# A SwiGLU layer's down projections issued one pair of up projections later, with the last one added on the vector engine

## The chip, the cores and the metric

The kernel runs on one core of one Trainium2 chip. A core has a tensor engine (PE; its weight loads are shown apart as PEld), a vector engine (DVE), a scalar engine (ACT), GpSimd (POOL) and SyncE (SP), which run side by side and wait for one another by semaphores; SP and POOL issue the DMAs here. The metric is the device time of one execution in microseconds (us), as the median of several.

## The reference

One decoder layer of 512 tokens, model width 1024 and FFN width 2816, all in float32. The change touches the two feed-forward parts, the first and the last of the four:

```python
def swiglu(x, w1, w3, w2):
    return (jax.nn.silu(x @ w1) * (x @ w3)) @ w2
...
h = layer_norm(ALPHA * h + 0.5 * swiglu(h, ffn1_w1, ffn1_w3, ffn1_w2), ln1_g, ln1_b)
h = layer_norm(ALPHA * h + parallel_mixer(h, ...), ln2_g, ln2_b)
h = layer_norm(ALPHA * h + memory_attention(h, mem, ...), ln3_g, ln3_b)
h = layer_norm(ALPHA * h + 0.5 * swiglu(h, ffn2_w1, ffn2_w3, ffn2_w2), ln4_g, ln4_b)
```

## The kernel before

**Numbers.** Each float32 operand is split into a high part (a CAST to fp32r) and a low part (source minus high part), so each weight tile costs a CAST of 128x1024 on ACT or DVE and a TENSOR_TENSOR of 128x1024 on DVE. One product of two split operands is three matmuls (`mm3`).

**The seven products.** The FFN width is cut into 22 tiles of 128, in 11 pairs. An **up unit** (`seven`) computes the gated activations G of a pair; a **down unit** (`down7`) multiplies four tiles, that is pairs 2g and 2g+1, by their rows of w2. Both are 2x2 block products done with seven block products in place of eight (a Strassen-Winograd scheme). An up unit is 7 products of 24 matmuls of 256 columns (tiles `pxwp`, `pzwp`, `pywp`), a down unit 7 products of 12 matmuls of 512 columns (`dx`, `dy`, `dz`). The weights of a product are formed on chip: four block additions on DVE (`wp_b`, `wd_b`) and seven splits per unit (`wp_hl`, `wd_hl`).

**Forms.** The other operand of a down product is a form `A1` to `A7` of G: blocks of G as they stand for 1, 2 and 4 (A1 from pair 2g, A2 and A4 from pair 2g+1), and the sums `Sa`, `Sb`, `Sc`, `Sd` for 5, 6, 3 and 7, each split like a weight. `Sa` is a block of pair 2g+1 minus one of pair 2g.

**Order of the work.** Pair 0 is done in plain form first, pair 10 goes through `res.add` (the last down projection, the residual and the layer norm; PE tile `res_w`). Between them, five groups: up 2g, up 2g+1, down g (group 0 has no first up). Down g therefore comes right behind the up unit whose G its forms A2 and A5 need.

**Accumulation.** A down unit's products leave PSUM through ACT (`st<-dx`, two copies for each result) and are added into four DRAM arrays `acc` by POOL's DMAs with accumulation; the first unit instead adds to the old residual on DVE and writes it by SP. Before `res.add` the sum is read back from DRAM into SBUF by eight SP DMAs (`load_acc`).

**Who decides the order on an engine.** PE's order follows the generators: each `yield` hands over to others, and what PE needs is pushed out before it. ACT, DVE and POOL get their rows from `Issue`, which keeps pending operations with a modelled cost and time and leaves the one whose data are due first; CASTs may go to ACT or DVE, whichever is modelled to end first. Weight splits get a delay of 4000 ns (`LATER`) in that due time. The order is fixed when the program is built. Split weights live in five buffers (`wsplit`), so the sixth is filled once the first was used.

The lines that set the groups and form A1 and A2 ahead of the down unit, and A5 and A6 at its start:

```python
        for g in range(5):
            if g:
                yield from seven(2 * g)
            forms = Forms(g)
            yield from seven(2 * g + 1, {4: lambda: forms.make(1, 2)})
            yield from down7(g, forms)
```

Of the kernel before, what the change touches and what calls it, by code (L numbers as in the profile page):

```python
# [13 lines left out]
ALU = mybir.AluOpType  # L14
# [180 lines left out]
def layer(ctx: ExitStack, tc: tile.TileContext, a: dict, out: bass.AP):  # L195
# [13 lines left out]
    act, dve, pool, sp = (Timed(issue, getattr(nc, e), e) for e in ("scalar", "vector", "gpsimd", "sync"))  # L209

    def slot(name, dtype=F32R, shape=None):
        return arena.tile(shape or [P, 2, 512], dtype, tag="slot", name=name)
# [39 lines left out]
    def split(hi, lo, src, scale=None):  # L252
        scaled(hi, src, scale)
        if scale is None:
            dve.tensor_tensor(lo, src, f32(hi), op=ALU.subtract)
        else:
            dve.scalar_tensor_tensor(lo, src, scale, f32(hi), op0=ALU.mult, op1=ALU.subtract)
# [105 lines left out]
    def project(name, w, toks=slice(None), o=0):  # L363

        ps = bank(name)
        for k in range(KT):
            mm3(ps, hl_of(w, slice(o + k * P, o + (k + 1) * P)), hk(k, toks), k == 0, k == KT - 1)
            if k % 2 and k < KT - 1:
                yield
        return ps  # L370
# [181 lines left out]
    def products(name, sums, out, late={}):  # L552

        def product(ps, i, first):
            late.get(i, lambda: None)()
            hl = W.take(f"{name}_{i}")
            for w in range(2):
                for k in range(4):  # L560
                    o = w * 512 + k * P
                    mm3(ps[:, w * 256:(w + 1) * 256], hl_of(hl, slice(o, o + P)), sums[i](k),
                        first and w == 0 and k == 0, w == 1 and k == 3, not first)
            W.done(f"{name}_{i}")

        x = bank(f"px{name}")
        product(x, 1, True)
        p1 = wk(f"p1_{name}")
        act.copy(p1, x)
        yield  # L570
        z = bank(f"pz{name}")
        product(z, 5, True)
        p5 = wk(f"p5_{name}")
        act.copy(p5, z)
        yield
        product(x, 6, False)
        u2 = wk(f"u2_{name}")
        act.copy(u2, x)
        yield
        product(z, 3, False)  # L580
        dve.tensor_tensor(u2, u2, z, op=ALU.add)
        drop(z)
        out(1, 0, u2, -1.0)
        yield
        product(x, 7, False)
        dve.tensor_tensor(p5, p5, x, op=ALU.add)
        out(1, 1, p5, -1.0)
        yield
        y = bank(f"py{name}")
        product(y, 2, True)  # L590
        dve.tensor_tensor(p1, p1, y, op=ALU.add)
        drop(y)
        out(0, 0, p1, 1.0)
        yield
        product(x, 4, False)
        out(0, 1, x, 1.0)
        drop(x)
        yield

    def plan_ffn(n, w1, w3, w2):  # L600
        for f in range(2):
            W.plan(f"w1_{n}_{f}", w1[f])
            W.plan(f"w3_{n}_{f}", w3[f])

        def up(p):
            return Unit(f"wp{n}_{p}", [[w[2 * p + i % 2][:, i // 2 * 512:i // 2 * 512 + 512] for w in (w1, w3)] for i in range(4)], ORDER)

        def down(g):
            return Unit(f"wd{n}_{g}", [[w2[f * P:(f + 1) * P, i % 2 * 512:i % 2 * 512 + 512] for f in (4 * g + i // 2 * 2, 4 * g + i // 2 * 2 + 1)]
                                       for i in range(4)], DOWN)  # L610

        units = [up(1), down(0)]
        for g in range(1, 5):
            units += [up(2 * g), up(2 * g + 1), down(g)]
        units.append(up(10))
        for u, v in zip(units, units[1:]):
            u.after = v
        for u in units:
            u.plan()
        for f in (20, 21):  # L620
            W.plan(f"w2_{n}_{f}", w2[f * P:(f + 1) * P])

    def ffn(n, src, ready=None):
        res = Residual(n, src)
# [7 lines left out]
        def gated(f, pa, pb):  # L632
            if f // 2 not in raw:
                raw[f // 2] = slot(f"G{n}_{f // 2}", F32)
            s = raw[f // 2][:, f % 2]
            act.activation(s, pa, AF.Silu)
            dve.scalar_tensor_tensor(s, pb, 0.5, s, op0=ALU.mult, op1=ALU.mult)
            drop(pa, pb)

        def up(fs):  # L640
            for f in fs:
                ps = []
                for w in ("w1", "w3"):
                    key = f"{w}_{n}_{f}"
                    ps.append((yield from project(f"p{key}", W.take(key))))
                    W.done(key)
                    yield
                gated(f, *ps)

        def seven(p, late=()):  # L650

            gated = raw[p] = slot(f"G{n}_{p}", F32)

            def out(c, half, ps, sign):
                dst = gated[:, c, 256 * half:256 * half + 256]
                act.activation(dst, ps[:, :256], AF.Silu, scale=sign)
                dve.scalar_tensor_tensor(dst, ps[:, 256:], 0.5 * sign, dst, op0=ALU.mult, op1=ALU.mult)
                if half and p == 10:
                    f = 2 * p + c
                    gT[f] = slot(f"g{n}_{f}")  # L660
                    split(gT[f][:, 0], gT[f][:, 1], gated[:, c])

            return products(f"wp{n}_{p}", sums, out, dict(late))
# [36 lines left out]
        def load_old():  # L700
            for h in range(2):
                for c in range(2):
                    t = old[h, c] = slot(f"old{n}_{h}_{c}", F32)
                    sp.dma_start(t, rows(src[256 * h:256 * h + 256, c * 512:c * 512 + 512]))

        def down7(g, forms):

            def product(pss, i, first):
                hl, x = W.take(f"wd{n}_{g}_{i}"), forms.hl.pop(i)
                for t in range(2):  # L710
                    for k in range(2):
                        mm3(pss[t], [x[:, k, j, t * P:(t + 1) * P] for j in (0, 1)], hl_of(hl, slice(k * 512, k * 512 + 512)),
                            first and k == 0, k == 1, not first)
                W.done(f"wd{n}_{g}_{i}")

            def add(pss, h, c, sign, new=False):
                if g == 0 and new:
                    st = old.pop((h, c))
                    for t in range(2):
                        dve.scalar_tensor_tensor(st[:, t], st[:, t], ALPHA, pss[t], op0=ALU.mult, op1=ALU.add if sign > 0 else ALU.subtract)  # L720
                    sp.dma_start(rows(acc[h, c]), st)
                else:
                    st = slot(f"st{n}_{g}_{h}_{c}", F32)
                    for t in range(2):
                        act.activation(st[:, t], pss[t], AF.Copy, scale=sign)
                    pool.dma_start(rows(acc[h, c]), st, accum_op=ALU.add)

            x = [bank(f"dx{n}_{g}_{t}") for t in range(2)]
            product(x, 1, True)
            add(x, 0, 0, 1.0, True)  # L730
            forms.make(5, 6)
            yield
            y = [bank(f"dy{n}_{g}_{t}") for t in range(2)]
            product(y, 2, True)
            add(y, 0, 0, 1.0)
            drop(*y)
            forms.make(3)
            yield
            z = [bank(f"dz{n}_{g}_{t}") for t in range(2)]
            product(z, 5, True)  # L740
            add(z, 1, 1, -1.0, True)
            forms.make(7)
            yield
            product(x, 6, False)
            add(x, 0, 1, -1.0, True)
            forms.make(4)
            yield
            product(z, 3, False)
            add(z, 0, 1, -1.0)
            drop(*z)  # L750
            yield
            product(x, 7, False)
            add(x, 1, 1, -1.0)
            yield
            product(x, 4, False)
            add(x, 1, 0, 1.0, True)
            drop(*x)
            yield
# [8 lines left out]
            mark = sums_of_h(n, sums)  # L767
            yield from up(range(2))
        yield mark
        load_old()  # L770
        for g in range(5):
            if g:
                yield from seven(2 * g)
            forms = Forms(g)
            yield from seven(2 * g + 1, {4: lambda: forms.make(1, 2)})
            yield from down7(g, forms)

        def load_acc():
            res.acc = [slot(f"acc{n}_{t}", F32, [P, D]) for t in range(NT)]
# [1 line left out]
                for c in range(2):  # L781
                    sp.dma_start(res.acc[t][:, c * 512:c * 512 + 512], acc[t // 2, c][t % 2 * P:t % 2 * P + P])

        yield from seven(10, {7: load_acc})
        yield from res.add(lambda i, t: hl_of(gT[20 + i], slice(t * P, (t + 1) * P)), [f"w2_{n}_{f}" for f in (20, 21)], False, True)


# [707 lines left out]
```

## Time and profile before

| | |
|---|---|
| median of 3 runs | 1308.88 us (1308.3 to 1309.8) |
| profiled execution, its own time | 1306.86 us |
| its span | 1305.0 us |
| mean granted clock of TensorE | 0.987 |
| PE busy | 1229.0 us, 94% of the span |
| DVE busy | 1038.6 us, 80% |
| ACT busy | 551.3 us, 42% |
| POOL busy | 99.4 us, 8% |

The busy shares are means over stages of different kinds. The first FFN runs from about 34 to 390 us, the second from about 955 us to the end; the mixer and the memory attention lie between and are not changed. A busy PE is one that has matmuls in flight; a gap between the records, with the name of what ended it, is a wait.

### The profile page before, as it was taken

Reading aid. Unit: us, or ns where it says so; the run is one execution under the profiler, and the core shown is the slowest. Engines: PE = TensorE matmul, PEld = TensorE weight load, DVE = VectorE, ACT = ScalarE, POOL = GpSimd, SP = SyncE. Lnnn points to the kernel's source line nnn. Section 1 sums busy time; section 2 is a strip of 40 time slices with the busy share of each in tenths; the row PEclk is TensorE's granted clock in tenths of the full one; section 3 lists DMA queues with packets and bytes.
Section 4 is the critical chain, followed back from the end, with each engine's and each line's share of the span. In section 5 each row is a group of like instructions: output and inputs, shape, how many; then the busy total and the mean of one; then the engine's idle time right before and its main releaser. Section 6 shows DMA issues by size and latency. Waiting matters only on the chain.

```text
span 1305.0 us, 19366 instructions
## 1 busy us (share of the span) xinstructions
PE 1229.0 (94%) x7530; PEld 1079.6 (83%) x7530; DVE 1038.6 (80%) x1603; ACT 551.3 (42%) x977; POOL 99.4 (8%) x95
## 2 busy tenths in 40 slices
PE   7898989899969999999999999999998989899995
PEld 6898988788859987877778898888996979797975
DVE  8999898789873699666666684574999898998987
ACT  5253434353532377433441243451544353535352
POOL 0010202020201100000000000000001020202020
PEclk9999999899989999999999999999999999999998
DMA  9381929484853321242333445234735474748374
GB/s 335 124 261 39 256 61 216 101 198 110 154 177 94 110 72 33 62 133 85 94 98 97 178 162 161 67 128 161 253 118 152 156 182 126 194 114 203 104 127 147
DMA packets 82879, 184.14 MB, mean 141 GB/s; under 512 B 8259, under 2 KB 10051, under 8 KB 82788
## 3 DMA queue, kind: packets, MB, share of 16 engines
q1 hardware_dynamic: 65924, 150.40, 34.3%
q0 software_dynamic: 16864, 32.51, 14.9%
q8 instruction: 59, 0.97, 0.3%
q14 instruction: 32, 0.26, 0.1%
HBM read 137.13 MB, written 45.74 MB: 140 GB/s over the span
## 4 chain that ended last, share of the span: by engine, by line
PE 70%; DVE 19%; DMA 4%; ACT 3%; issue 3%; SPq 0%; POOL 0%; DVEq 0%; POOLq 0%; ACTq 0%
PE pxwp L260 13%; PE pzwp L260 7%; DVE wd_hl L178 6%; PE dx L260 6%; PE dz L260 4%; PE mq L260 3%; PE res_w_o L260 3%; PE pgd L260 3%; PE res_mem_w_o L260 3%; DVE wd_b L178 2%; PE pywp L260 2%; PE pw L260 2%; PE mk L260 2%; PE vd L260 2%; PE pw_gm L260 2%
## 5 line engine op out<-in xcount | busy, mean ns | idle before, releaser
L178 DVE TENSOR_TENSOR wp_hl<-wp_b,wp_hl 128x1024 fp32r<-128x1024 f32 x140 | 168.9, 1222 | 15.6 <-ACT wp_hl L178 14.7
L178 ACT CAST wp_hl<-wp_b 128x1024 fp32r<-128x1024 f32 x88 | 92.1, 1052 | 82.1 <-PE pxwp L260 34.9
L260 PE MATMUL dx<-wd_hl,A 128*128 128x512 f32 x480 | 121.7, 399 | 2.4 <-DVE A L178 1.1
L170 POOL DMA_DIRECT2D acc<-st x62 | 77.6, 1478 | 600.5 <-ACT st L178 435.1
L260 PE MATMUL pxwp<-hT,wp_hl 128*128 128x256 f32 x960 | 121.1, 282 | 1.1 <-ACT wp_hl L178 0.4
L260 PE MATMUL pzwp<-S,wp_hl 128*128 128x256 f32 x960 | 121.8, 283 | 0.3 <-DVE S L178 0.3
L260 PE MATMUL pxwp<-S,wp_hl 128*128 128x256 f32 x960 | 122.0, 283 | 0.0
L260 PEld LDWEIGHTS pxwp<-hT,wp_hl 128*128 128x128 f32 x960 | 117.1, 188 | 5.5 <-DVE p_wp L178 2.1
L260 PEld LDWEIGHTS pzwp<-S,wp_hl 128*128 128x128 f32 x960 | 117.9, 191 | 0.5 <-DVE S L178 0.5
L260 PEld LDWEIGHTS pxwp<-S,wp_hl 128*128 128x128 f32 x960 | 118.1, 191 | 0.2 <-ACT p_wp L178 0.2
L260 PEld LDWEIGHTS dx<-wd_hl,A 128*128 128x128 f32 x480 | 88.9, 190 | 26.6 <-DVE A L178 7.6
L178 DVE TENSOR_TENSOR wd_hl<-wd_b,wd_hl 128x1024 fp32r<-128x1024 f32 x70 | 85.0, 1223 | 16.5 <-ACT wd_hl L178 16.3
L178 DVE TENSOR_TENSOR wp_b<-wp_b,wp_b 128x1024 f32<-128x1024 f32 x80 | 97.5, 1221 | 0.3
L260 PE MATMUL dz<-wd_hl,A 128*128 128x512 f32 x240 | 62.6, 400 | 12.2 <-ACT A L178 12.2
L260 PEld LDWEIGHTS dz<-wd_hl,A 128*128 128x128 f32 x240 | 43.7, 189 | 27.4 <-ACT A L178 15.9
L260 PE MATMUL pywp<-hT,wp_hl 128*128 128x256 f32 x480 | 60.0, 280 | 0.3 <-ACT wp_hl L178 0.3
L260 PE MATMUL dy<-wd_hl,A 128*128 128x512 f32 x120 | 37.1, 460 | 22.7 <-ACT A L178 17.7
L260 PEld LDWEIGHTS pywp<-hT,wp_hl 128*128 128x128 f32 x480 | 58.0, 188 | 0.5 <-ACT wp_hl L178 0.5
L260 PE MATMUL pw<-hT,w_hl 128*128 128x256 f32 (+1 forms) x288 | 50.2, 335 | 6.6 <-ACT hT L178 6.4
L260 PEld LDWEIGHTS pw<-hT,w_hl 128*128 128x128 f32 x288 | 43.0, 197 | 13.1 <-ACT hT L178 7.1
L260 PEld LDWEIGHTS dy<-wd_hl,A 128*128 128x128 f32 x120 | 24.9, 219 | 34.2 <-ACT A L178 21.5
L178 ACT ACTIVATE st<-dx 128x512 f32<-128x512 f32 x68 | 39.8, 598 | 22.9 <-PE dx L260 22.7
(329 smaller groups left out, 2332.0 us busy)
## 6 DMA issues: line engine op xcount, KB each, us to landing
wp_b<-in_ffn_w SPq DMA_DIRECT2D x160, 256.0 KB, 5.6
acc<-st POOLq DMA_DIRECT2D x62, 512.0 KB, 9.5
wd_b<-in_ffn_w SPq DMA_DIRECT2D x80, 256.0 KB, 6.8
h_dram<-acc SPq DMA_DIRECT2D x12, 512.0 KB, 3.0
w_raw<-in_ffn_w SPq DMA_DIRECT2D x11, 512.0 KB, 5.0
w_gm_raw<-in_w_gate SPq DMA_DIRECT2D x8, 512.0 KB, 5.8
acc<-old SPq DMA_DIRECT2D x8, 512.0 KB, 4.2
acc<-acc SPq DMA_DIRECT2D x16, 256.0 KB, 5.6
```

The lines of the kernel that those rows point to most:

```text
L170: return (name, 1000.0, 4000.0, lambda: getattr(engine, op)(*args, **kw)), args[:1], list(args)
L178: return (name, ns, 1500.0 if name == "sync" else 0.0, lambda: getattr(engine, op)(*args, **kw)), outs, ins
L260: issue.pe(lambda: nc.tensor.matmul(ps, w, x, start=start, stop=stop, skip_group_check=again), ps, w, x)
```

## The change

Down unit g is issued one pair of up units later. Before, the order was up 1, down 0, up 2, up 3, down 1, ..., up 9, down 4, up 10; now it is up 1, up 2, down 0, up 3, up 4, down 1, ..., up 9, up 10, down 4. The planned order of the weights follows. The forms A1, A2 and A5 are now made at products 3, 2 and 4 (the fourth, sixth and seventh in the order 1, 5, 6, 3, 7, 2, 4) of the up unit ahead of the down unit, and need the G of up units that ended earlier. In the last group the residual is read back ahead of that up unit's first product, and the seven results of down 4 are added to it in SBUF by DVE directly from PSUM: 14 additions of 128x512 in each FFN, in place of 14 ACT copies and 7 accumulating POOL DMAs.

```diff
-        units = [up(1), down(0)]
-        for g in range(1, 5):
-            units += [up(2 * g), up(2 * g + 1), down(g)]
-        units.append(up(10))
+        units = []
+        for g in range(5):
+            units += [up(2 * g + 1), up(2 * g + 2), down(g)]
...
             def add(pss, h, c, sign, new=False):
-                if g == 0 and new:
+                if g == 4:
+                    for t in range(2):
+                        dst = res.acc[2 * h + t][:, c * 512:c * 512 + 512]
+                        dve.tensor_tensor(dst, dst, pss[t], op=ALU.add if sign > 0 else ALU.subtract)
+                elif g == 0 and new:
...
             add(x, 0, 0, 1.0, True)
-            forms.make(5, 6)
+            forms.make(6)
...
-        load_old()
-        for g in range(5):
-            if g:
-                yield from seven(2 * g)
-            forms = Forms(g)
-            yield from seven(2 * g + 1, {4: lambda: forms.make(1, 2)})
-            yield from down7(g, forms)
...
-        yield from seven(10, {7: load_acc})
+        load_old()
+        for g in range(5):
+            yield from seven(2 * g + 1)
+            forms = Forms(g)
+            late = {3: lambda: forms.make(1), 2: lambda: forms.make(2), 4: lambda: forms.make(5)}
+            if g == 4:
+                late[1] = load_acc
+            yield from seven(2 * g + 2, late)
+            yield from down7(g, forms)
```

**PE at the start of down 2 of the second FFN** (names carry the FFN, the unit and a buffer number; x23 is a run of 23 like rows). Before, the last product of up 5 ends and `dx`, `dy` follow:

```order
L260 MATMUL pywp4_5_10513<-hT1_90,wp4_5_2_hl_10381 128x256 x21
L260 MATMUL pxwp4_5_10356<-hT1_90,wp4_5_4_hl_10419 128x256 [waits DVE_49]
L260 MATMUL pxwp4_5_10356<-hT1_90,wp4_5_4_hl_10419 128x256 x23
L260 MATMUL dx4_2_0_10584<-wd4_2_1_hl_10449,A1_4_2_10551 128x512 [waits DVE_49]
L260 MATMUL dx4_2_0_10584<-wd4_2_1_hl_10449,A1_4_2_10551 128x512
L260 MATMUL dx4_2_1_10585<-wd4_2_1_hl_10449,A1_4_2_10551 128x512 x2
L260 MATMUL dx4_2_0_10584<-wd4_2_1_hl_10449,A1_4_2_10551 128x512 [waits DVE_49]
L260 MATMUL dx4_2_0_10584<-wd4_2_1_hl_10449,A1_4_2_10551 128x512 x3
L260 MATMUL dx4_2_1_10585<-wd4_2_1_hl_10449,A1_4_2_10551 128x512 x4
L260 MATMUL dy4_2_0_10619<-wd4_2_2_hl_10478,A2_4_2_10552 128x512 [waits PE_49,Activation_49]
L260 MATMUL dy4_2_0_10619<-wd4_2_2_hl_10478,A2_4_2_10552 128x512
```

Now:

```order
L260 MATMUL pywp4_6_10728<-hT1_90,wp4_6_2_hl_10593 128x256 x21
L260 MATMUL dx4_2_0_10804<-wd4_2_1_hl_10661,A1_4_2_10666 128x512
L260 MATMUL dx4_2_0_10804<-wd4_2_1_hl_10661,A1_4_2_10666 128x512 [waits DVE_49]
L260 MATMUL dx4_2_0_10804<-wd4_2_1_hl_10661,A1_4_2_10666 128x512 x4
L260 MATMUL dx4_2_1_10805<-wd4_2_1_hl_10661,A1_4_2_10666 128x512 x6
L260 MATMUL dy4_2_0_10836<-wd4_2_2_hl_10691,A2_4_2_10729 128x512 [waits DVE_49,Activation_49]
L260 MATMUL pxwp4_6_10568<-hT1_90,wp4_6_4_hl_10631 128x256 [waits DVE_49]
L260 MATMUL pxwp4_6_10568<-hT1_90,wp4_6_4_hl_10631 128x256 x23
L260 MATMUL dy4_2_0_10836<-wd4_2_2_hl_10691,A2_4_2_10729 128x512 x5
L260 MATMUL dy4_2_1_10837<-wd4_2_2_hl_10691,A2_4_2_10729 128x512 [waits PE_49]
L260 MATMUL dy4_2_1_10837<-wd4_2_2_hl_10691,A2_4_2_10729 128x512 x5
L260 MATMUL dz4_2_0_10862<-wd4_2_5_hl_10721,A5_4_2_10770 128x512 [waits Activation_49]
```

The down unit now follows up 6, while its forms are of pairs 4 and 5. The whole first down product stands ahead of the last up product `pxwp4_6`, which waits for DVE.

**DVE at the same place.** Before, from the last rows of G of pair 5 to the low part of A5:

```order
L178 SCALAR_TENSOR_TENSOR G4_5_10355<-p1_wp4_5_10384,G4_5_10355 128x256 [waits Activation_49]
L178 CAST wd4_2_7_hl_10598<-wd4_2_b1_10315 128x1024 [waits DVE_49,PE_49]
L178 SCALAR_TENSOR_TENSOR G4_5_10355<-pxwp4_5_10356,G4_5_10355 128x256
L178 TENSOR_TENSOR A2_4_2_10552<-G4_5_10355,A2_4_2_10552 128x2x256 [waits DMASW0_49,Activation_49]
L178 TENSOR_TENSOR wd4_2_7_hl_10598<-wd4_2_b1_10315,wd4_2_7_hl_10598 128x1024 [waits DVE_49]
L178 TENSOR_TENSOR wd4_2_b0_10314<-wd4_2_b0_10314,wd4_2_b2_10383 128x1024
L178 TENSOR_TENSOR Sa_4_2_10602<-G4_5_10355,G4_4_10130 128x512 [waits DVE_49]
L178 CAST wd4_2_4_hl_10633<-wd4_2_b0_10314 128x1024 [waits DVE_49,PE_49]
L178 TENSOR_TENSOR Sd_4_2_10661<-G4_4_10130 128x512
L178 TENSOR_TENSOR A5_4_2_10603<-Sa_4_2_10602,A5_4_2_10603 128x2x256 [waits Activation_49]
```

Now, from the addition `u2` of up 6 to the low part of A5:

```order
L178 TENSOR_TENSOR u2_wp4_6_10662<-u2_wp4_6_10662,pzwp4_6_10606 128x512 [waits Activation_49]
L178 TENSOR_TENSOR wd4_2_5_hl_10721<-wd4_2_b0_10526,wd4_2_5_hl_10721 128x1024 [waits DVE_49]
L178 SCALAR_TENSOR_TENSOR G4_6_10567<-u2_wp4_6_10662,G4_6_10567 128x256 [waits Activation_49]
L178 TENSOR_TENSOR wd4_2_b0_10526<-wd4_2_b0_10526,wd4_2_b3_10594 128x1024 [waits DMAHW7_49,DMAHW1_49,DVE_49]
L178 TENSOR_TENSOR A2_4_2_10729<-G4_5_10342,A2_4_2_10729 128x2x256 [waits Activation_49]
L178 TENSOR_TENSOR p5_wp4_6_10632<-p5_wp4_6_10632,pxwp4_6_10568 128x512
L178 TENSOR_TENSOR wd4_2_6_hl_10754<-wd4_2_b0_10526,wd4_2_6_hl_10754 128x1024 [waits Activation_49]
L178 TENSOR_TENSOR p1_wp4_6_10596<-p1_wp4_6_10596,pywp4_6_10728 128x512
L178 SCALAR_TENSOR_TENSOR G4_6_10567<-p5_wp4_6_10632,G4_6_10567 128x256 [waits Activation_49]
L178 TENSOR_TENSOR wd4_2_3_hl_10795<-wd4_2_b3_10594,wd4_2_3_hl_10795 128x1024 [waits PE_49]
L178 TENSOR_TENSOR A5_4_2_10770<-Sa_4_2_10769,A5_4_2_10770 128x2x256 [waits DMASW1_49]
```

`Sa` (now seven rows above the first of these) and A2 no longer stand behind a G that was made just before, and the high part of A5 is on ACT ahead of the CAST of `wd4_2_6`. ACT takes most of the CASTs of the down weights: of the 70 CASTs of `wd` DVE had 41 and has 14.

**DVE at the end of the first FFN.** Before, from the split of the last w2 tile to the splits of `g`, the gated activations of pair 10 (`w_gm` are the mixer's first weights):

```order
L178 CAST g1_21_3456<-G1_10_3302 128x512 [waits DVE_49]
L178 TENSOR_TENSOR p1_wp1_10_3329<-p1_wp1_10_3329,pywp1_10_3471 128x512 [waits PE_49]
L178 TENSOR_TENSOR g1_21_3456<-G1_10_3302,g1_21_3456 128x512 [waits DVE_49]
L178 TENSOR_TENSOR w_gm1_hl_3497<-w_gm1_raw_3496,w_gm1_hl_3497 128x1024 [waits DMAHW5_49,Activation_49]
L178 SCALAR_TENSOR_TENSOR G1_10_3302<-p1_wp1_10_3329,G1_10_3302 128x256 [waits Activation_49]
L178 TENSOR_TENSOR w_gm2_hl_3530<-w_gm2_raw_3529,w_gm2_hl_3530 128x1024 [waits DMAHW6_49,Activation_49]
L178 SCALAR_TENSOR_TENSOR G1_10_3302<-pxwp1_10_3303,G1_10_3302 128x256 [waits Activation_49]
L178 CAST g1_20_3531<-G1_10_3302 128x512 [waits DMASW2_49,DVE_49]
L178 TENSOR_TENSOR g1_20_3531<-G1_10_3302,g1_20_3531 128x512 [waits DVE_49]
```

Now, down 4's additions (`acc<-acc,dx` and so on), between which the same weights are split, ahead of the residual's additions:

```order
L178 TENSOR_TENSOR w2_1_21_hl_3456<-w2_1_21_raw_3455,w2_1_21_hl_3456 128x1024 [waits Activation_49]
L178 TENSOR_TENSOR acc1_3_3128<-acc1_3_3128,dx1_4_1_3370 128x512 [waits DVE_49,PE_49]
L178 TENSOR_TENSOR w_gm0_hl_3478<-w_gm0_raw_3477,w_gm0_hl_3478 128x1024 [waits Activation_49]
L178 TENSOR_TENSOR acc1_0_3125<-acc1_0_3125,dz1_4_0_3418 128x512 [waits DVE_49]
L178 TENSOR_TENSOR acc1_1_3126<-acc1_1_3126,dz1_4_1_3419 128x512 [waits DVE_49]
L178 TENSOR_TENSOR w_gm1_hl_3499<-w_gm1_raw_3498,w_gm1_hl_3499 128x1024 [waits DMAHW7_49,Activation_49]
L178 TENSOR_TENSOR acc1_2_3127<-acc1_2_3127,dx1_4_0_3369 128x512 [waits DMAHW1_49,PE_49]
L178 TENSOR_TENSOR w_gm2_hl_3518<-w_gm2_raw_3517,w_gm2_hl_3518 128x1024 [waits DMAHW0_49,Activation_49]
L178 TENSOR_TENSOR acc1_3_3128<-acc1_3_3128,dx1_4_1_3370 128x512 [waits DMAHW2_49]
L178 SCALAR_TENSOR_TENSOR acc1_0_3125,sums1_0_3525<-acc1_0_3125,res1_w2_1_20_0_0_3526 128x512 [waits PE_49]
```

The splits of `g` moved ahead of down 4's first additions; the splits of `w_gm` stand between its last ones. On SP, the eight loads of `acc` stand behind the loads of down 4's weights and ahead of `lng`, `lnb` and `w_gm_raw`; before, `w_gm_raw` followed them directly and `lng` and `lnb` came later.

## Rows read from the trace of the kernel before

**Rows 1.** Timeline of PE, 1132 to 1197: start, length, what, [idle before <-releaser].

```profile
1132.18 3.02 PE L260 MATMUL pxwp<-hT,wp_hl 128*128 128x256 f32 x24
...
1172.49 1.07 PE L260 MATMUL dx<-wd_hl,A 128*128 128x512 f32 x4
...
1177.57 3.05 PE L260 MATMUL dy<-wd_hl,A 128*128 128x512 f32 x12 [1.75 <-ACT A L178]
1182.03 3.21 PE L260 MATMUL dz<-wd_hl,A 128*128 128x512 f32 x12 [1.41 <-ACT A L178]
...
1190.96 5.42 PE L260 MATMUL dx<-wd_hl,A 128*128 128x512 f32 x23
1196.22 1.00 PE L260 MATMUL pxwp<-hT,wp_hl 128*128 128x256 f32 x7
```

**Rows 2.** The critical chain before that `dz`: start, length, what.

```profile
1180.67 0.61 DVE Sa L178
...
1181.36 0.63 ACT A L178
```

**Rows 3.** Windows: length; busy of PE, PEld, DVE, ACT, POOL; clock, DMA share, GB/s.

```profile
33.70:100.20 66.50, 62.84 (x422) 57.38 (x422) 62.62 (x78) 27.01 (x39) 3.75 (x3) 0.95 0.62 196
100.20:164.30 64.10, 60.65 (x423) 55.34 (x422) 57.94 (x71) 27.52 (x44) 8.86 (x7) 1.00 0.59 144
228.40:298.80 70.40, 65.48 (x431) 59.40 (x432) 58.63 (x74) 32.40 (x48) 8.97 (x7) 0.93 0.65 158
954.80:1024.20 69.40, 62.68 (x423) 56.35 (x422) 65.21 (x81) 27.40 (x39) 3.67 (x3) 0.98 0.52 153
1132.35:1196.39 64.04, 60.65 (x422) 55.32 (x422) 58.66 (x70) 27.63 (x45) 8.86 (x7) 1.00 0.61 155
```

**Rows 4.** Waits of DVE, 1132.35 to 1196.39: us in total, times, longest.

```profile
DVE wd_hl L178 <- ACT wd_hl L178: 2.0, 1, 2.0
DVE wp_hl L178 <- ACT wp_hl L178: 1.6, 1, 1.6
DVE wp_hl L178 <- PE dx L260: 1.0, 1, 1.0
DVE wp_hl L178 <- PE pzwp L260: 0.5, 1, 0.5
```

**Rows 5.** Timeline of DVE and, last, of ACT, 1163 to 1184.

```profile
1173.57 0.68 DVE L178 TENSOR_TENSOR p_wp<-p_wp,pywp 128x512 f32<-128x512 f32 x1
1174.17 1.22 DVE L178 TENSOR_TENSOR wd_hl<-wd_b,wd_hl 128x1024 fp32r<-128x1024 f32 x1
...
1176.78 0.69 DVE L178 CAST wd_hl<-wd_b 128x1024 fp32r<-128x1024 f32 x1
...
1172.69 1.05 ACT L178 CAST wd_hl<-wd_b 128x1024 fp32r<-128x1024 f32 x1 [2.72 <-PE pxwp L260]
```

**Rows 6.** Waits of PE, 228.4 to 298.8: us in total, times, longest.

```profile
PE dy L260 <- DVE A L178: 1.8, 1, 1.8
PE dy L260 <- DVE wd_hl L178: 1.6, 1, 1.6
```

**Rows 7.** End of the first FFN: timelines of PE, DVE and SP's queue.

```profile
369.78 10.10 PE L260 MATMUL res_w<-w_hl,g 128*128 128x512 f32 x36 [6.80 <-DVE g L178]
...
366.23 1.23 DVE L178 TENSOR_TENSOR w_gm_hl<-w_gm_raw,w_gm_hl 128x1024 fp32r<-128x1024 f32 x1 [4.42 <-ACT w_gm_hl L178]
...
337.85 21.25 SPq L178 DMA_DIRECT2D acc<-acc  x8
```

**Rows 8.** Waits of PE, 1196.39 to 1305, at the second FFN's end.

```profile
PE res_w L260 <- DVE g L178: 1.4, 1, 1.4
```

**Rows 9.** Page, part 6: DMA issues, KB each, median us to landing.

```profile
acc<-st POOLq DMA_DIRECT2D x62, 512.0 KB, 9.5
...
acc<-acc SPq DMA_DIRECT2D x16, 256.0 KB, 5.6
```

**Rows 10.** Timeline of POOL's queue, 318 to 362: one down unit's last accumulations.

```profile
346.05 3.70 POOL L170 DMA_DIRECT2D acc<-st  x3 [9.14 <-DMA acc<-st]
```

## The prediction

> **What bounds the kernel now.** I read the page first, then PE's timeline over one group of the second FFN (two up units and a down unit), the waits and the critical chain there, windows for every group, and last the ends of the two FFNs.
>
> In the timeline [rows 1] the two up units run from 1132.18 to 1172.49 without a gap, 40.31 us. The down unit runs from 1172.49 to 1196.22, 23.73 us. Its last 23 matmuls took 1196.22 - 1190.96 = 5.26 us, 0.229 each, so its 84 matmuls without waiting need 19.2 us. PE's floor for a group is 40.3 + 19.2 = 59.5 us; the group took 64.04 [rows 3], so it loses 4.5 us, all in the down unit. Most of that is two gaps [rows 1]: `dy` starts after 1.75 us of waiting for ACT's CAST of A2, `dz` after 1.41 us for A5. What was late is told by the chain ahead of `dz` [rows 2]: DVE makes `Sa` at 1180.67, ACT casts it at 1181.36, PE starts at 1182.03. Both forms need the G of the up unit that just ended, and that G sits in DVE's queue between splits of 1.22 us.
>
> DVE is almost as full as PE: 58.66 of 64.04 us in that group [rows 3], with 5.1 us of waits [rows 4].
>
> **The change, part by part.**
>
> *The forms.* Down g now uses pairs whose G ended a whole up unit (20 us) earlier. `Sa`, A1, A2 and A5 wait for no fresh result any more, and their rows stand ahead of the end of the up unit. The two gaps of rows 1 and the rest of the 4.5 us should go, unless something else is late next.
>
> What can be late next is DVE itself, because its work per group hardly changes. From rows of the order: per down unit 2.7 CASTs of `wd` less (41 to 14 over ten units), and over ten units 9 more CASTs of A and 5 more of `wp`; at 0.69 us for a CAST of 1024 [rows 5] and something over half of that for one of 512, that is about 1 us less per group: 57.7 us. Of DVE's waits, the 2.0 us for ACT's CAST of `wd_hl` lies in the crowded stretch at the down unit's start and should shrink; the other three (1.6, 1.0 and 0.5) have nothing to do with the forms, and I keep them: 3.1. So DVE needs 57.7 + 3.1 = 60.8 us for a group, a little over PE's floor, and it is DVE that sets the new period. Gain 64.04 - 60.8 = 3.2 us per group. The bounds are 4.5 (PE's floor) and 0.
>
> A new wait lies at the same place. PE does the first down product ahead of the last up product `pxwp`, which waits for `p_wp+=pxwp` on DVE behind three splits or additions of 1.22 us. Counting DVE's rows from the end of the fifth up product, that addition ends about 5.4 us later; PE meanwhile has `pywp` and the first `dx` product (12 x 0.229 = 2.7 us), together 5.6 us. So it just fits. ACT's CAST of `wd_3` waits for a buffer that PE frees, as it does today (2.72 us of idle behind `pxwp` [rows 5]), and three G activations queue behind it; in most groups the buffer is now freed by that first `dx`, some 3 us before the up unit ends. Continuing the count, the low part of A5 is done at 9.4 us and PE wants it at 11.2; A6 is the tightest, 15.1 against 14.9.
>
> Groups 1 and 2 of the first FFN and 1, 2 and 3 of the second are of this kind: 5 x 3.2 = 16.
>
> *The first groups.* They took 66.5 and 69.4 us, with DVE busy 62.62 and 65.21 [rows 3]: the sums of h are split there, so DVE is the limit and only its idle 3.9 and 4.2 us can be won. I take 1.5 each, 3 in all (bounds 0 and 8).
>
> *Group 3 of the first FFN.* It took 70.4 us with DVE busy only 58.63 [rows 3]: other work of DVE (tables for the mixer) delays the down weights, and `dy` waits 1.8 us for A and 1.6 us for `wd_hl` [rows 6]. Down to 60.8 it would give 9.6; its weights are still behind other rows in the new order, so I take under half, 4.5 (bounds 0 and 9.6).
>
> *The ends.* The wait of `res_w` for g, 6.80 us in the first FFN [rows 7] and 1.4 in the second [rows 8], goes, since g is split before down 4 starts. So does the loss in down 4 (4.5 each). Against that stand 14 additions of 128x512 in each FFN. The nearest row is `p_wp+=pywp`, the same operation from PSUM: 0.68 us, and 0.60 from start to start [rows 5]; 14 x 0.60 = 8.4 us if all lie on the path, nothing if they lie in the room that the next up unit's weights leave (there is no next one). In the first FFN the 4.42 us that DVE waits for ACT's CAST of `w_gm` [rows 7] are kept, because `lng` and `lnb` now stand ahead of those loads on SP and the splits still stand ahead of the residual's additions. First FFN: between 11.3 - 8.4 - 4.4 = -1.5 and 11.3 - 4.4 = +6.9; second: between 5.9 - 8.4 = -2.5 and +5.9. I take +1 and 0, nearer the lower ends, because an addition stands in DVE's order behind 1.22 us splits and PE reuses the same bank. ACT's 28 copies and POOL's 14 accumulations that go were off the path and count nothing; if ACT were late again they would count 0.6 each.
>
> *The residual's loads.* The eight SP loads wait for POOL's accumulations today for 21.25 us [rows 7], with `w_gm` behind them. Now they come ahead of up 10, a full up unit after down 3, behind down 4's weights on SP; an accumulation lands 9.5 us after its issue and a load in 5.6 [rows 9], and a down unit's chain ends with three issues after a wait of 9.14 us for the one before [rows 10], so the loads should end some 25 us after down 3, while the first addition comes after 40. Nothing is counted.
>
> Sum: 16 + 3 + 4.5 + 1 = 24.5 us off the profiled 1306.86, 1282.4. The median of the runs is 2.0 above the profiled execution: **1284 us**.
>
> A rule of the Trainium skill speaks against this. "Perfetto Trace Analysis", section "Identifying the Most-Contended Engine", says to rank DVE by its occupancy and PE by LDWEIGHTS busy, and to relieve the higher one first. In the group at 100.20 that ranks DVE (57.94 of 64.10) over PEld (55.34) [rows 3], and the change gives DVE 28 operations more. By that rule there would be no gain, which is the second rival.
>
> **The rivals.**
>
> 1. *PE's floor.* DVE's remaining waits shrink too, and a group takes 59.5: 5 x 4.5 = 22.5, 8 in the first groups, 10.9 in group 3, and the ends give their upper bounds, 12.8: 54 us, 1255 at the extreme, some 1265 with half of what is uncertain. For it: PE has no gap in up units. Against: DVE would have to idle under 2 us of 59.5.
>
> 2. *DVE is the bound already.* The gaps move from A to the weights: PE waits the same 4.5 us per group for `wd_hl` or `pxwp`, and only group 3 and the ends give something, 0 to 6: 1302 to 1309. For it: occupancy of 91%. Against: 5.1 us of waits, 2.0 of them at the very place.
>
> 3. *Slower: the additions.* If DVE is the bound and in down 4 each pair of additions holds PSUM, so that PE stops for it, both ends lose the 8.4 us, and the groups give nothing: 1308.9 + 16.8 = 1326. It decides where the additions of a product end later than the next product that writes that bank is due, 2.7 us on. For it: four products of `dx` share two banks. Against: before, ACT's copies had the same deadline at 0.6 each.
>
> **How the numbers follow.** My forecast, 1276 to 1296, has 0.58; rival 1 has 0.14; rival 2 has 0.20, of which a quarter lies within 0.2% (about what a measurement of this kernel can tell from no change); rival 3 has 0.08. Faster 0.58 + 0.14 + 0.15 = 0.87, same 0.05, slower 0.08. The range leaves out rival 3, the lower half of rival 1 and the slower end of rival 2: 1266 to 1304.
>
> **What would show it.** Right: `dy` and `dz` without a wait for ACT's A; groups of 60 to 62 us, DVE busy above 94% in them; no `res_w` wait of 6.8 us, first residual addition of the second FFN at much the same distance from the last product. Wrong: `pxwp` (the last up product) or `dx` waiting for DVE by 3 us or more per group (rival 2), gaps in down 4 named after `acc` (rival 3), or a longer stretch from down 4 to the mixer's first matmul through `w_gm`.

## The result and the profile after

The changed kernel takes 1278.87 us (median of 4, 1278.29 to 1279.87) against 1309.08 us (1308.3 to 1309.8) for the kernel before, run beside it: a ratio of 0.977, 95% interval 0.9753 to 0.9787, or 30.2 us. The forecast was 1284. The profiled execution went from 1306.86 to 1278.71 us, its span from 1305.0 to 1276.9, and the span's 28.1 us are what the rows below account for.

PE's timeline at the same place as [rows 1], the start of a down unit of the second FFN in the new order:

```profile
1169.35 0.39 PE L260 MATMUL dy<-wd_hl,A 128*128 128x512 f32 x1
1169.57 3.02 PE L260 MATMUL pxwp<-hT,wp_hl 128*128 128x256 f32 x24
1172.43 2.66 PE L260 MATMUL dy<-wd_hl,A 128*128 128x512 f32 x11
1174.93 2.88 PE L260 MATMUL dz<-wd_hl,A 128*128 128x512 f32 x12
1177.65 2.60 PE L260 MATMUL dx<-wd_hl,A 128*128 128x512 f32 x9
```

The gaps of 1.75 and 1.41 us ahead of `dy` and `dz` are gone; PE lists no wait from 1047.3 to 1226.3, three whole groups. Windows that answer to [rows 3], each from the start of one down unit to the start of the next; the fourth is down 4 of the second FFN alone, the last the span from down 2 to down 3 of the first:

```profile
985.26:1047.29 62.03, 60.78 (x423) 55.74 (x421) 60.40 (x76) 27.55 (x41) 3.67 (x3) 1.00 0.53 162
1047.29:1106.71 59.42, 59.42 (x423) 55.89 (x421) 56.56 (x68) 29.27 (x46) 8.76 (x7) 1.00 0.67 169
1106.71:1166.58 59.87, 59.67 (x423) 55.78 (x422) 57.37 (x70) 28.86 (x46) 8.52 (x7) 1.00 0.67 168
...
1226.34:1254.16 27.82, 25.74 (x116) 20.50 (x114) 26.85 (x39) 10.28 (x15) 0.00 (x0) 0.94 0.10 38
...
190.66:265.34 74.68, 67.25 (x450) 61.28 (x449) 56.84 (x75) 31.08 (x48) 8.87 (x7) 0.93 0.64 146
```

A group of 64.04 us is now one of 59.4 to 59.9, about the 59.5 that the prediction gives as PE's floor, and PE is busy through it (59.67 of 59.87 us). DVE is busy 57.4 of 59.9 us. DVE's waits in the window from 1106.71, to be held against [rows 4]:

```profile
DVE wp_hl L178 <- ACT wp_hl L178: 1.2, 1, 1.2
DVE wd_hl L178 <- ACT wd_hl L178: 0.9, 1, 0.9
```

Of 5.1 us of waiting 2.1 are left: the three waits that were to stay have shrunk (1.6 to 1.2) or gone (1.0 and 0.5). Two places lost time. PE's and SP's timelines in group 3 of the first FFN:

```profile
223.38 2.30 PE L260 MATMUL rel<-hot,rel 33*8 33x320 f32 x4 [7.32 <-DMA hot<-in_onehot]
```

```profile
201.63 11.06 SPq L178 DMA_DIRECT2D wp_b<-in_ffn_w  x8
212.80 0.64 SPq L178 DMA_DIRECT2D hot<-in_onehot  x1
```

`hot` is the one-hot table from which PE makes the mixer's bias table. Its load stands on SP behind eight weight loads, which wait for buffers, and the matmul stands on PE at the place where the builder's clock put it; PE, now ahead, stood there for 7.32 us. What followed ran slowly as well: TensorE's granted clock was 0.51 of full speed, its level of 1.2 GHz, and the 24 `pzwp` matmuls from 225.61 took 5.27 us to issue, where a like row takes 2.88.

```profile
223.40:231.00 7.60, 7.60 (x29) 5.74 (x30) 2.01 (x4) 1.49 (x2) 3.07 (x3) 0.51 0.94 139
```

The other place is the first FFN's end, here in windows of before (the first two lines) and of after:

```profile
342.80:362.90 20.10, 20.10 (x169) 19.95 (x167) 15.53 (x19) 5.43 (x9) 3.70 (x3) 1.00 0.83 194
362.90:380.00 17.10, 10.18 (x37) 7.89 (x36) 9.39 (x18) 3.84 (x6) 0.57 (x1) 0.80 0.55 180
```

```profile
327.69:354.71 27.02, 24.25 (x115) 19.25 (x114) 26.84 (x39) 12.04 (x17) 0.00 (x0) 1.00 0.20 65
354.71:366.00 11.29, 9.91 (x44) 7.88 (x42) 10.69 (x24) 4.71 (x6) 0.56 (x1) 1.00 0.46 148
366.00:381.00 15.00, 7.67 (x33) 6.47 (x33) 14.92 (x24) 6.47 (x13) 2.56 (x3) 0.55 0.50 186
```

Before, DVE had room in up 10 (15.53 of 20.10) and in the stretch of `res_w` (9.39 of 17.10); now it is full from down 4's start to the mixer's first matmul. The 6.80 us of [rows 7] are gone, but PE waits for DVE's `acc` ahead of the transposes (`trh`) instead. PE's waits from 326.75 to 383:

```profile
PE trh L269 <- DVE acc L178: 8.7, 4, 3.0
PE res_w L260 <- DVE acc L178: 1.5, 1, 1.5
PE dx L260 <- DVE acc L178: 1.2, 2, 0.6
```

Where the 28.1 us are, from the starts of down units (`dx`) in both timelines. The marks do not stand at the same point of the work, and the column "after" is set right for that. The new order has one up unit more ahead of a mark (20.15 us, half of the two in [rows 1]); but that unit's last product, the `pxwp` at 1169.57 in the first timeline above, stands behind the mark, 2.86 us. So 17.29 us are taken off the pieces that begin with a first up unit, and added to those that begin with a fifth down unit:

| piece | before | after | gain | forecast |
|---|---|---|---|---|
| four full groups (one in the first FFN, three in the second) | 64.04, 64.01, 64.09, 64.05 | 59.38, 59.42, 59.87, 59.76 | 17.8 | 12.8 |
| first up unit to the second down unit, both FFNs | 86.9, 89.7 | 81.8, 83.4 | 11.3 | 3 |
| first FFN, third to fifth down unit | 134.7 | 137.0 | -2.4 | 7.7 |
| first FFN, fifth down unit to the mixer's first matmul | 70.2 | 70.5 | -0.3 | 1 |
| second FFN, fifth down unit to the end | 68.4 | 67.8 | 0.6 | 0 |
| start of the kernel, and between the FFNs | | | 1.1 | 0 |

The last line is no gain of the change: the first up unit starts at 32.1 us in this trace, at 33.5 in that of before, and between 33.1 and 34.5 in those of all the experiments.

In the first groups, too, the waits for forms went, and they had been the longest ones. PE's rows of down 0 before, in the first FFN and in the second, and a window over the first:

```profile
59.96 5.79 PE L260 MATMUL dy<-wd_hl,A 128*128 128x512 f32 x12 [3.45 <-ACT A L178]
981.07 1.19 PE L260 MATMUL dy<-wd_hl,A 128*128 128x512 f32 x4 [2.11 <-ACT A L178]
983.89 3.47 PE L260 MATMUL dy<-wd_hl,A 128*128 128x512 f32 x8 [1.64 <-DVE A L178]
989.50 3.05 PE L260 MATMUL dz<-wd_hl,A 128*128 128x512 f32 x12 [2.14 <-ACT A L178]
60.00:65.50 5.50, 5.50 (x12) 3.93 (x13) 5.50 (x9) 1.11 (x2) 0.00 (x0) 0.50 0.25 95
```

These are 9.3 us of waiting, and behind the gap of 3.45 us the granted clock was 0.50: the next product, a `dz` at 65.55, starts 5.59 us after that `dy` product began, where twelve such matmuls need 2.7. In the new order down 0 has no listed wait for A, and the granted clock is 1.00 (first window above).

### The profile page after: what moved, and what is told of

The parts are those of the page before. It is cut to its first block, busy times and chain, and to the rows that moved or that the text cites. A ratio compares the mean times of both kernels' runs of the same rounds, so it can differ in the third digit from the quotient of the medians.

```text
span 1276.9 us, 19369 instructions
## 1 busy us (share of the span) xinstructions
PE 1224.6 (96%) x7530; PEld 1083.8 (85%) x7530; DVE 1039.0 (81%) x1613; ACT 552.7 (43%) x967; POOL 80.7 (6%) x81
## 4 chain that ended last, share of the span: by engine, by line
PE 77%; DVE 16%; ACT 2%; issue 2%; DMA 2%; POOL 0%; SPq 0%; DVEq 0%; POOLq 0%; ACTq 0%
PE pxwp L260 15%; PE pzwp L260 9%; PE dx L260 7%; PE pywp L260 4%; PE mq L260 4%; PE res_w_o L260 3%; PE pgd L260 3%; PE res_mem_w_o L260 3%; PE pw_gm L260 2%; PE dz L260 2%; PE pw L260 2%; PE mk L260 2%; PE vd L260 2%; PE qd L260 2%; PE kd L260 2%
## 5 line engine op out<-in xcount | busy, mean ns | idle before, releaser
L260 PE MATMUL pzwp<-S,wp_hl 128*128 128x256 f32 x960 | 124.7, 287 | 0.9 <-DVE S L178 0.5
L178 ACT CAST wp_hl<-wp_b 128x1024 fp32r<-128x1024 f32 x83 | 86.3, 1050 | 89.8 <-PE pxwp L260 54.7
L170 POOL DMA_DIRECT2D acc<-st x48 | 59.4, 1539 | 516.3 <-ACT st L178 267.5
L178 ACT CAST wd_hl<-wd_b 128x1024 fp32r<-128x1024 f32 x52 | 54.2, 1051 | 69.2 <-DVE wd_b L178 37.6
L260 PE MATMUL pywp<-hT,wp_hl 128*128 128x256 f32 x480 | 60.8, 280 | 0.3 <-ACT wp_hl L178 0.3
L178 DVE TENSOR_TENSOR wd_b<-wd_b,wd_b 128x1024 f32<-128x1024 f32 x40 | 48.6, 1218 | 0.0
L260 PE MATMUL pgd<-hT,w_gd_hl 128*128 128x512 f32 x192 | 47.5, 400 | 0.0
```

Of the source, the lines that this page charges most:

```text
L170: return (name, 1000.0, 4000.0, lambda: getattr(engine, op)(*args, **kw)), args[:1], list(args)
L178: return (name, ns, 1500.0 if name == "sync" else 0.0, lambda: getattr(engine, op)(*args, **kw)), outs, ins
L260: issue.pe(lambda: nc.tensor.matmul(ps, w, x, start=start, stop=stop, skip_group_check=again), ps, w, x)
```

## The experiments

The kernel before ran beside each set (1308.4 to 1309.6 us); the ratios are to it.

**The two halves of the change, apart.** The new order with the old way out of the last down unit:

```diff
-                if g == 4:
-                    ... (additions into res.acc on DVE)
-                elif g == 0 and new:
+                if g == 0 and new:
...
-            if g == 4:
-                late[1] = load_acc
...
             yield from down7(g, forms)
+        load_acc()
         yield from res.add(...)
```

> The new order of the units alone: the last down unit again leaves PSUM through ACT and POOL's accumulating DMAs, and the residual is read back behind it. Theory (the gain of the groups comes from the forms being one pair old; the additions in SBUF only keep the order payable at the ends): the groups keep their 59.4 to 62 us, but each FFN's end now waits for POOL's chain (about 15 us from the last product to the last landing) and for the loads (6 us) in the open, so 1310 to 1322 us. Rival (the 14 additions per FFN cost their 8.4 us on the path, so that without them the ends get faster): 1262 to 1275 us.

Measured: 1303.1 us, 0.9951 (0.9934 to 0.9967), between the two ranges. The groups are those of the changed kernel (59.43, 59.47, 59.75, 59.83). Both ends pay, less than expected: PE's and DVE's rows, of the first and the second FFN:

```profile
380.15 3.68 PE L269 MATMUL trh<-ident,acc 128*128 128x128 f32 x16 [18.02 <-DVE acc L178]
```

```profile
1273.01 0.69 DVE L178 SCALAR_TENSOR_TENSOR acc<-acc,res_w 128x512 f32<-128x512 f32 x1 [13.55 <-DMA acc<-acc]
```

From the fifth down unit on, this kernel is 11.4 us behind the changed one in the first FFN (to the mixer's first matmul) and 13.2 in the second. So the order brings the gain and the additions in SBUF keep 24 us of it from being lost; the rival is out.

The other half, in the old order (the same `add`, and `load_acc` at up 9's first product):

> The old order of the units, with the last down unit's results added in SBUF by the vector engine and the residual read back one unit earlier. Theory: groups stay at 64 us and dy and dz still wait for ACT's A; the first FFN's end gets back most of the 6.8 us before res_w, against which stand additions beside the splits of up 10's weights: 1302 to 1310 us. Rival (the gain came from this part): under 1295 us.

Measured: 1314.86 us, 1.004 (1.0025 to 1.0055): slower, beyond the 1302 to 1310 that were expected. PE waits for the forms as before:

```profile
PE dy L260 <- ACT A L178: 17.8, 9, 3.5
PE dz L260 <- ACT A L178: 12.6, 8, 2.1
PE res_w L260 <- DVE g L178: 5.2, 2, 3.8
```

The wait of `res_w` shrinks (8.2 us in both FFNs before), yet from the fifth down unit on the first FFN is 2.5 us longer than before and the second 3.6. Alone, the additions gain nothing; in the new order the same additions are worth 24 us.

**Fresh G, or early rows.** The forms of the changed kernel, made where the old one made them:

```diff
-            late = {3: lambda: forms.make(1), 2: lambda: forms.make(2), 4: lambda: forms.make(5)}
+            late = {4: lambda: forms.make(1, 2)}
...
-            forms.make(6)
+            forms.make(5, 6)
```

> The changed kernel, with the forms made at the old places (1 and 2 at the last product of the up unit, 5 and 6 at the start of the down unit); they are still of pairs that ended a unit earlier. Theory (what counted was that the form's G was fresh): most of the gain stays, 1279 to 1290 us. Rival (what counted is that the forms are issued earlier): dy and dz wait for A again, 1297 to 1310 us.

Measured: 1290.82 us, 0.9858 (0.9843 to 0.9873). It lies just above the theory's range and below the rival's: 18 of the 30 us stay, 12 go. `dy` waits for no A and `dz` for 3.4 us in all; the lost part is another wait of PE:

```profile
PE pxwp L260 <- DVE p_wp L178: 14.1, 9, 1.8
```

This is the wait that the prediction found to "just fit". With A1 made at the last product, the first down product no longer goes as a whole ahead of the last up product (in most groups no matmul of it does), so nothing covers the time in which `p_wp+=pxwp` waits behind DVE's splits: 1.6 us in nine of ten groups, and full groups of 61.2 us in the second FFN.

**CASTs.** The planner had also moved 27 CASTs from DVE to ACT. In the kernel before:

```diff
-            split(hl[:, 0], hl[:, 1], src)
+            if self.order == DOWN and i not in (2, 5):
+                act.copy(hl[:, 0], src)
+                dve.tensor_tensor(hl[:, 1], src, f32(hl[:, 0]), op=ALU.subtract)
+            else:
+                split(hl[:, 0], hl[:, 1], src)
```

> The kernel before, with five of the seven CASTs of each down unit's weights put on ACT (50 of 70, as in the changed kernel; 25 before). Rival (the groups gained because DVE was relieved of 27 CASTs, about 16 us): 1291 to 1298 us. Theory (the groups waited for forms, and DVE is not the bound): groups stay at 64 us, 1305 to 1315 us.

Measured: 1302.18 us, 0.9947 (0.9931 to 0.9963): neither. It is worth 6 us, with full groups of 63.0 us but for one of 63.9. PE's waits in the whole run, and the window of one group:

```profile
PE dy L260 <- DVE A L178: 20.2, 16, 3.5
...
PE dz L260 <- DVE A L178: 1.9, 2, 1.6
```

```profile
1106.77:1169.78 63.01, 60.71 (x422) 55.43 (x421) 57.38 (x71) 29.34 (x44) 8.96 (x7) 1.00 0.63 159
```

The edit did not relieve DVE as far as meant: the planner moved 32 CASTs of A from ACT to DVE in return, and DVE's busy time over the run fell by 8 us (1038.6 to 1030.9), not 16. What can be compared is a group: DVE is busy 57.38 us in it, as much as in the changed kernel (57.37), and it takes 63.0 us in place of 59.9. So DVE's load is worth about 1 of the 4.5 us that a group lost, and the rest comes with the order. The wait ahead of `dz` (12.2 us in the kernel before) is nearly gone and the one ahead of `dy` stays; whether `dz` gained by the CASTs of `wd` or by those of A, which need no other engine now, is not shown.

**DVE's room in a group.** Four and eight more operations were put into each of three down units:

```diff
+            def extra(count):
+                if n == 4 and 0 < g < 4:
+                    for _ in range(count):
+                        dve.tensor_tensor(mask, mask, mask, op=ALU.max)
```

> The changed kernel with four more DVE operations of 128x512 (about 2.4 us) in each down unit of groups 1 to 3 of the second FFN. They read and write a tile that no later result needs. Theory (PE is at its floor of 59.5 us there, DVE busy 57.4 and with about 2 us to spare): 0 to 3 us slower than the changed kernel, 1279 to 1282 us. Rival (DVE sets the period): 7.2 us slower, 1286 us.

> As the run with four more operations, but eight (about 4.8 us) in each of the three down units. Theory: DVE passes PE, 3 times 2.5 to 3 us, 1285 to 1289 us. Rival (DVE sets the period already): 14.4 us slower, 1293 us.

Measured: 1277.84 and 1283.45 us. Neither tells anything of DVE's room: the operations did not stay where they were put. The trace of the run with eight has them ahead of the second FFN, up to 561.6 us (operation, shortest, median, longest ns, first and last start):

```profile
L178 DVE TENSOR_TENSOR mask<-mask x24: 673/692/695, 531.1 to 561.6; 128x512 f32<-128x512 f32 x24
```

Nothing they read or write tied them to the second FFN. Still the run with eight has two groups of 60.8 and 63.3 us there, with 3.6 us in which `dx` waits for ACT's copy `st`: a plan laid out anew moves a group by this much with no load in it. In the next two runs the operations were tied to the two forms A1 and A2, `k` = 2 and 4 for each, that is four and eight in a group:

```diff
                     split(t[:, :, 0], t[:, :, 1], x)
+                    if n == 4 and 0 < self.g < 4 and i in (1, 2):
+                        for _ in range(k):
+                            dve.tensor_tensor(t[:, :, 1], x, f32(t[:, :, 0]), op=ALU.subtract)
```

> The changed kernel; in groups 1 to 3 of the second FFN the low parts of A1 and A2 are computed three times in place of once, the same values again: four DVE operations of 128x512 more in each group, 2.4 us, at a place where their rows can't leave the group. The prediction's step was that DVE needs 60.8 us for a group and so sets its period. By that step the run is 3 x 2.4 = 7 us slower than the changed kernel, 1286 us. Theory now (PE is at its floor of 59.5 us there, and DVE, busy 57.4, has about 2.5 us to spare): groups of 59.5 to 60.5 us, 1278 to 1282 us.

> As the run with four more DVE operations in each group, but eight, 4.8 us. Prediction's step: 14.4 us slower than the changed kernel, 1293 us. Theory now: DVE passes PE and groups take 61.5 to 63 us, 1284 to 1290 us.

Measured: 1289.79 and 1284.45 us; the smaller load cost more than the larger, and more than either of its two forecasts. The three groups took 192.2 and 184.7 us together, where the changed kernel takes 179.05. The planner, with other durations to sum, had again laid the rows out anew (in the run with four operations 57 CASTs of A are on ACT in place of 50), and in the run with four operations a chain like this one, ACT's row first, then PE's, cost 7.2 us in three waits:

```profile
1138.05 0.60 ACT L178 ACTIVATE st<-dx 128x512 f32<-128x512 f32 x1 [3.28 <-DMA acc<-st]
```

```profile
1138.70 4.60 PE L260 MATMUL dx<-wd_hl,A 128*128 128x512 f32 x12 [1.85 <-ACT st L178]
```

ACT's copy waits for POOL's accumulation to free its slot, and PE for the copy. In the run with eight operations that wait was 2.3 us, and 14.4 us of extra work cost 5.7. DVE was busy in its three windows 178.9 us of 184.7, 7.7 more than in the changed kernel, because the planner moved CASTs to ACT. That 1284.45 lies in the range expected of a full DVE shows nothing, then: these runs do not tell how much room DVE has. What is shown is that PE has none: it is busy 178.7 of the 179.05 us of the changed kernel's three groups.

**The additions' price.** Each of the 28 additions done as two, with another operation that can halve the value:

```diff
-                        dve.tensor_tensor(dst, dst, pss[t], op=ALU.add if sign > 0 else ALU.subtract)
+                        for _ in range(2):
+                            dve.scalar_tensor_tensor(dst, pss[t], 0.5 * sign, dst, op0=ALU.mult, op1=ALU.add)
```

> The changed kernel with each of the 28 additions into the residual done as two, half of the value each time: 28 operations of 128x512 more, 16.8 us. Theory (DVE is full in the last down unit, so additions lie on the path there): 10 to 17 us slower than the changed kernel, 1289 to 1296 us. Rival (they are hidden because no next unit's weights are split then): under 4 us slower, up to 1283 us.

Measured: 1293.58 us, 0.9875 (0.9859 to 0.9891): 14.7 us more than the changed kernel, 0.53 for an addition. In the traces the two ends are longer by 8.9 and 5.2 us, 0.50 for an addition. They lie on the path almost in full.

**The table's load.** The loads of `hot` and of `lam` are issued first, and what reads them follows 15 us of the builder's clock later:

```diff
+        sp.dma_start(room[:, :256], a["lam"].partition_broadcast(P))
+        mark = Mark()
+        mark.floor = issue.clock + 15000.0
+        yield mark
         rows = arena.tile([8, REL], F32, tag="slot", name="rows")
```

> The changed kernel, with the loads for the mixer's tables (the one-hot table and lam) issued some 15 us ahead of the first matmul and DVE operation that read them. In the changed kernel PE stood 7.3 us for the one-hot table in group 3 of the first FFN. Theory (PE stood only for the load, DVE having caught up by then): 5 to 8 us faster than the changed kernel, 1271 to 1274 us. Rival (the wait only covers another, DVE's splits of the down weights being late there anyway): 1277 to 1280 us.

Measured: 1271.73 us, 0.9709 (0.9693 to 0.9725), 7.1 us below the changed kernel, as the theory had it. Third to fifth down unit: 129.6 us in place of 137.0. The wait for `hot` is gone; the next group gives some back (66.19 in place of 62.35). With a lead of 30 us, begun 15 us earlier:

> The changed kernel with the table loads 30 us ahead of their use (and begun 15 us earlier) in place of 15. With 15, PE's 7.3 us were gone, but DVE stood 2.4 us for lam, and group 3 of the first FFN kept 4 us of waits for A and 2.2 for the sum ahead of the last up product. Theory (those came from DVE having been held by that load): 3 to 6 us faster than with 15 us of lead, 1266 to 1269 us. Rival (group 3 lacks DVE time whatever the loads): within 2 us of it, 1270 to 1274 us.

Measured: 1269.72 us, 0.97 (0.9685 to 0.9714), 2.0 us below the run with 15 us of lead. That lies between the two ranges, and the intervals overlap. The trace shows some of both: third to fifth down unit take 126.5 us in place of 129.6, and the wait of 2.2 us for the sum ahead of the last up product is gone; but `dy` still waits 2.3 us for DVE's A and 1.7 for ACT's, with no wait of DVE for a load left in that piece.

**A faster version.** On top of that, the first two results of the last down unit leave by ACT and by accumulating DMAs, into the residual in SBUF, which takes 8 of the 28 additions off DVE:

```diff
+                if g == 4 and dma:
+                    st = slot(f"st{n}_{g}_{h}_{c}", F32)
+                    for t in range(2):
+                        act.activation(st[:, t], pss[t], AF.Copy, scale=sign)
+                        pool.dma_start(res.acc[2 * h + t][:, c * 512:c * 512 + 512], st[:, t], accum_op=ALU.add)
```

> As the run with 30 us of lead, and of the seven results of the last down unit the first two (8 of 28 additions) leave PSUM by ACT's copies and are added into the SBUF residual by POOL's accumulating DMAs. Theory (an addition on DVE at the ends costs about 0.53 us of the run, 14.7 us for 28 more): 3 to 5 us faster than without it. Rival (both DMAs go to the same bytes, one after the other, about 10 us each, and the last addition of the residual now waits for them): 0 to 8 us slower.

Measured: 1264.81 us, 0.9663 (0.9649 to 0.9677), 4.9 us below the run beside it, or 0.6 for an addition. In the traces the ends account for 3.1 of it: 1.8 us up to the mixer's first matmul and 1.3 in the second FFN. This version beats both kernels.

## Why the prediction was right, step by step

**The forms: right.** `dy` and `dz` wait for no A any more, and the order alone does it. The claim that the other forms' rows would be tight was right too: A6 was to be late by 0.2 us, and that `dx` product, at 1117.75, takes 3.28 us in place of 2.88.

**The new wait: right, and worth more than a remark.** "So it just fits" holds in the changed kernel, where `pxwp` has no listed wait for `p_wp`; the run with late forms shows what stands behind it, 14 us.

**DVE sets the period at 60.8: wrong, in size and in what sets it.** The term that failed is the 3.1 us of waits that were kept as having "nothing to do with the forms". Together with the 2.0 of the CAST they came to 2.1 in all, so DVE needs 57.4 + 2.1 = 59.5, no more than PE. PE is busy through the groups, so they stand at its floor, and a group gives 4.4 in place of 3.2; whether DVE could have gone faster is open. That DVE would need about 1 us less per group was a little low: it went from 58.66 to between 56.6 and 57.4. By a miscount the text and the section on the change gave 41 and 14 CASTs of `wd` on DVE; the trace has 45 and 18, with the same difference, and 8 CASTs of A more, not 9.

**The first groups: wrong, 3 for 11.3 us.** The step said that DVE is the limit there and that only its idle time in the window can be won. But what PE stood for in those windows were forms again, 3.45 us in the first FFN and 5.9 in the second, and in both the granted clock fell behind the gaps (0.50 from 60 to 65.5, 0.54 from 984 to 987.3). The prediction read DVE's share for these windows and not PE's waits. DVE was 97% busy after as well (60.40 of 62.03 in the second FFN, window above), with PE waiting for little more than 1 us. The gain lay outside the bounds (0 to 8).

**Group 3 of the first FFN: wrong sign, 7.7 forecast with the group behind it, -2.4 measured.** This is the largest error. The down weights were no longer late, but a load that had landed in time before was waited for now: 7.32 us for `hot`, with the slow clock behind it. The section on the change does not name it and no rival did. With 15 us of lead for the load the piece gives 5.1, and with 30 it gives 8.2, about the forecast.

**The ends: +1 forecast and +0.3 measured, but not by its terms.** The wait of `res_w` went as foreseen, and the additions, on a DVE that is full there, cost 0.50 to 0.53 of their 0.60 us. The 4.42 us that DVE was to go on waiting for ACT's CAST of `w_gm` are wrong, though; DVE's waits from 327.69 to 381 have

```profile
DVE w_gm_hl L178 <- ACT w_gm_hl L178: 0.4, 1, 0.4
```

In their place stand two losses that were in no term: the waits of `trh` (8.7 us, against 3.6 before) and the slow clock behind them (last section). That the sum came out is luck. The residual's loads cost nothing, as said: no wait for them is listed.

**The sum: in part luck.** The pieces missed by +5.0 (full groups), +8.3 (first groups), -10.1 (the piece with group 3), -0.7 (ends) and +1.1 (start and middle), and 24.5 became 28.1 because the two largest misses nearly cancel.

**The rivals.** PE's floor (rival 1) is what the full groups reached, and the first groups gave more than its 8, though not group 3 and the ends. DVE as the bound already (rival 2) fails in the groups: DVE's busy time in the whole run is 1038.6 us before and 1039.0 after, and the time fell by 30. The rule of the Trainium skill that spoke for it ("Perfetto Trace Analysis", section "Identifying the Most-Contended Engine") ranks DVE by its occupancy; the trace does not bear it out here, since the lost time was a chain through DVE and ACT, which were busy 58.66 and 27.63 of the 64.04 us of a group. Rival 3's sign, gaps named after `acc` in down 4, is there at 4.4 us in both FFNs together (`dx`, `dz` and `res_w`), in place of 16.8, and the groups gave what it denied.

## What to carry to other kernels

If a unit's operands come from the unit just before it, each step through another engine's queue is paid in the open; issue it one unit later, and make the operands early enough that the unit's first product can also cover waits of its neighbour. Bound a gain by the waits of the engine that waits, not by another engine's idle time in the same window: here that bound said 8 us where 9.3 us of waits and a slow clock behind them could go. When two orders of work are held against each other, check that the marks stand at the same point of the work. And after a speedup, look at what was placed by a fixed time (a table, a load): it was in time only because the others were late.

## What had not been expected

A mean addition from PSUM at a full DVE costs the run nearly its start-to-start time: 0.50 to 0.53 us of 0.60. Accumulating DMAs from SBUF into SBUF took the place of eight of them, and from the fifth down unit on both ends were shorter, by 1.8 and 1.3 us; in the first FFN's end the waits of `trh` for `acc` grew (7.5 to 9.8 us, the longest 7.6), but those inside down 4 went. In the changed kernel's first FFN's end TensorE's granted clock was 0.55 between 366 and 381 us, with waits for DVE ahead of and between the transposes, and a run of eight transposes took 1.97 us where it takes 1.09 in the kernel before, some 3.5 us over the four runs; how much of that lies on the path was not taken apart.
